# A later gate group's last plain unit becomes a seventh Strassen unit, and the turned results get their low parts from ScalarE and adding transfers

## The chip, the cores and the metric

The kernel runs on one core of one Trainium2 chip. The metric is the time of the program on the device, in microseconds (us), as the median of several runs. The profile is one further execution, recorded by the hardware profiler. The engines are called by the profile's names: PE (TensorE: matmuls; PEld is its weight load), DVE (VectorE), ACT (ScalarE), POOL (GpSimd, here mostly a place from which transfers are issued) and SP (SyncE, which issues the loads).

## The reference, cut to what matters

One layer of a decoder trunk: 256 tokens, width 2048, all numbers float32. The change touches only the feed-forward part, of width `D_FF` = 5632:

```
f = rmsnorm(h, ffn_norm[i])
h = h + (jax.nn.silu(f @ w_gate[i]) * (f @ w_up[i])) @ w_down[i]
```

Ahead of it stand an input projection, two kinds of attention and an output projection; behind it a gated embedding (`w_ple_gate`, `w_ple_proj`) and a last norm.

## The kernel before, in words

**Products in three matmuls.** Each factor is split into a high part (the number rounded to the fp32r type) and a low part (what the rounding left). A product is three matmuls: high by high, low by high, high by low (`three`, L385). The low part of a weight block is read by the third alone. The high part of a weight block is cast by ScalarE (L337), the low part is made by VectorE as raw minus high (L348).

**Groups and units.** The feed-forward part goes through six chunks of 1024 columns of `w_gate` and `w_up`. For each chunk there is a gate group (`g0` to `g4`), an up group (`u0` to `u4`) and, one chunk later, two groups of `w_down` (`d1` to `d4`, each for half of the output columns, which I write d20 and d21 for chunk 2). The sixth chunk is narrower and does gate and up in one group, `gu5`. The order is g0, u0, g1, d10, u1, d11, g2, d20, u2, d21, g3 and so on to d41, gu5, and then the last two groups of `w_down`. A group is a list of units, each of 256 rows of the weight (a *pair* of 128-row tiles), 1024 columns wide.

**Plain and Strassen units.** A plain unit is 2 row tiles x 2 column chunks x 2 token tiles x 3 = 24 matmuls of 128x512. A unit marked `S` in `mixed` (L1080) does the same in seven block products instead of eight (Strassen's scheme in Winograd's form): 7 x 3 = 21 matmuls, in four *turns* of 6, 3, 6 and 6 (`seven`, L442). It needs the four blocks of the weight and four sums of them: VectorE makes the sums in place (L347, L350, L351) and low parts of seven blocks instead of four. The blocks are named "11 22", "21", "t1 t3" and "t4 t2": two, one, two and two blocks of 512 columns, one name for each turn. Within turn 0 they are used by products m1 and m3, in turn 1 by m2, in turn 2 by m7 and m5, in turn 3 by m6 and m4. Three of the seven (m2, m3, m4) add straight to the result banks (0,0), (1,0) and (0,1), where the plain units' products lie too, as they do in the fourth, (1,1); m1, m5, m6 and m7 have a bank each, and VectorE puts them together in the tile `U` after the last Strassen unit (L465 to L469).

**Order before.** `mixed` lists the units: `6 S0 S1 S2 S3 S4 S5 7` for g1 to g4 and gu5, `S0 S1 S2 S3 S4 S5 S6 7` for u1 to u4. The four result banks are copied to the tile `stage` by ScalarE after the last plain unit (`gate_add`, L1012), and an adding transfer from POOL adds `U` to them (L1018).

**The ring.** Casted blocks live in 20 places of 512 columns (12 in `ring`, 4 in `more`, 4 in `most`), filled in turn; `plan` (L232) gives each block its place and notes which turn last reads it. A block must not straddle places 12 or 16. The main loop (L1382 to L1425) issues the casts of later units before each turn's matmuls, as far ahead as the loads, three units at most, and the ring allow: a block whose place is read by turn n is issued at turn n + 1 at the earliest. `high_parts` issues ScalarE's casts, then `step` runs one piece of each waiting task, then `split` issues the rest. Each engine carries its instructions out in the order in which they are issued.

**The middle of the first plain unit.** The chunk's result (gate times up, in `stage`) has to be turned before `w_down` can use it. This is done in the first plain unit of the next gate group: half of the unit's matmuls, then 16 transposes on PE into the four spare banks (`ff_transpose`, L1041), then the other half. Before, each bank was cast by ScalarE (L106) and its low part taken by VectorE (L107), and the four banks were then free for m1, m7, m5, m6 of the first Strassen unit. Blocks that could have been issued ahead of this (`late`) were issued behind it.

Of the kernel before, what the change touches and what calls it, by code (L numbers as in the profile page):

```python
# [13 lines left out]
ALU = mybir.AluOpType  # L14
# [21 lines left out]
def kernel(ctx, tc, x, w_in, w_ukv, w_o, w_gate, w_up, w_down, w_ple_gate, w_ple_proj,  # L36
# [137 lines left out]
    def group(name, srcs, ks, chunks, lhs, evac, pool=None, singles=0, per=2, sums=None, sevens=(), adding=(),  # L174
              order=None, swap=False, bank0=0, deep=False, into=None, early=(), keep=False):

        pairs = [ks[i:i + 1] for i in range(singles)] + [ks[i:i + per] for i in range(singles, len(ks), per)]
        st = {"banks": None, "begun": set()}
        for i, pr in enumerate(pairs):
            u = Unit()  # L180
            u.name, u.srcs, u.ks, u.chunks, u.lhs, u.st = name, srcs, pr, chunks, lhs, st
            u.first, u.last, u.evac, u.pool = i == 0, i == len(pairs) - 1, evac, pool
            u.order = order or [(c, t) for c in range(len(chunks)) for t in range(NT)]
            u.idx, u.store, u.again, u.into = i, None, None, into
            u.strassen, u.sevens_first, u.sevens_end = i in sevens, i in sevens[:1], i in sevens[-1:]
            u.mixed, u.sums, u.swap, u.bank0, u.deep, u.adding = len(sevens) > 0, sums, swap, bank0, deep, i in adding
            u.early, u.keep = i in early, keep
            units.append(u)

    raw = {}  # L190
# [213 lines left out]
    def product(u, kks, between=()):  # L404

        end = u.last and kks[-1] == len(u.ks) - 1
        take_banks(u)
        parts = u.parts if not u.again else units[u.again].parts
        for c, t in u.order:
            if c == "keys":  # L410
                b = u.st["banks"][c, t]
                for kk in kks:
                    for i in range(2):
                        w = [x[:, (2 * t + i) * 128:(2 * t + i + 1) * 128] for x in parts[kk]]
                        three(b[:, i * SEQ:(i + 1) * SEQ], w, *(x[:, u.ks[kk], :] for x in S["ckvT"]),
                              begins(u, (c, t)), end and kk == kks[-1] and i == 1)
                if end:
                    u.evac(c, t, 0, 512, b)
                continue
            c0, c1 = u.chunks[c]  # L420
            b = u.st["banks"][c, t][:, 0:c1 - c0]
            for kk in kks:
                h, l = parts[kk]
                three(b, u.lhs(u.ks[kk], t), h[:, c0:c1], l[:, c0:c1], begins(u, (c, t)), end and kk == kks[-1])
            if end:
                if u.mixed and u.into is None and not isinstance(u.evac, partial):
                    us = S["U"][:, t, c0:c1]
                    nc.vector.tensor_tensor(us, us, b, op=ALU.add)
                    u.evac(c, t, c0, c1, us)
                else:  # L430
                    u.evac(c, t, c0, c1, b)
                if between and (c, t) == u.order[0]:
                    split(between.pop(0))
        if end and u.mixed and not u.keep:
            B["acc"], B["rot"], B["next"] = u.st["free"], [u.st["banks"][ct] for ct in u.order], 0
        elif end and u.swap:
            swap_banks()
# [4 lines left out]
    def seven(u, turn):  # L442
        st = u.st
        if turn == 0 and u.sevens_first:
            take_banks(u)
            n = B["next"] % 4
            st["free"] = B["rot"][n:] + B["rot"][:n]
            B["rot"], B["next"] = [st["banks"][1, 1]] if u.first else [], 0
            st.update(zip(("m1", "m7", "m5", "m6"), st["free"]))
        h, l = u.turns[turn][0].h, u.turns[turn][0].l  # L450
        k = u.ks[0]
        a11, a12, a22 = u.lhs(k, 0), u.lhs(k + 1, 0), u.lhs(k + 1, 1)
        s1, s2, s3, s4 = (u.sums(k, j) for j in range(4))
        todo = (((0, "m1", a11), (1, "m3", s4)), ((0, "m2", a12),), ((1, "m7", s3), (0, "m5", s1)),
                ((1, "m6", s2), (0, "m4", a22)))[turn]
        alone = {"m2": (0, 0), "m3": (1, 0), "m4": (0, 1)}
        for q, m, xs in todo:
            b = st["banks"][alone[m]] if m in alone else st[m]
            three(b, xs, h[:, 512 * q:512 * q + 512], l[:, 512 * q:512 * q + 512], begins(u, alone.get(m, m)),
                  u.sevens_end and m not in alone)  # L460
        if turn == 3 and u.sevens_end:
            U = S["U"] = big.tile([128, NT, 1024], F32, name="U", tag="vb")
            c1, c2 = U[:, :, 0:512], U[:, :, 512:1024]
            tt = nc.vector.tensor_tensor
            nc.scalar.copy(c1[:, 0], st["m1"])  # L465
            tt(c2[:, 0], c1[:, 0], st["m6"], op=ALU.add)
            tt(c1[:, 1], c2[:, 0], st["m7"], op=ALU.add)
            tt(c2[:, 0], c2[:, 0], st["m5"], op=ALU.add)
            tt(c2[:, 1], c1[:, 1], st["m5"], op=ALU.add)  # L469
            B["rot"], B["next"] = st["free"], 0  # L470
            if u.into is not None:
                def join(hs=S["h"][:, :, u.into:u.into + 1024]):
                    tt(hs, hs, U, op=ALU.add)
                    yield 1
                add(join())
# [536 lines left out]
    def gate_add(ci, c, t, c0, c1, b):  # L1012

        if "ff" not in S:
            S["ff"] = stage_tile(1024)
        nc.scalar.copy(S["ff"][:, t, c0:c1], b)
        if (c, t) == (1, 1):
            nc.gpsimd.dma_start(S["ff"], S["U"], accum_op=ALU.add)  # L1018

            def silu():  # L1020
                for i in range(NT):
                    nc.scalar.activation(S["ff"][:, i], S["ff"][:, i], AF.Silu, scale=S["rf"][:, i:i + 1])
                yield 1
            add(silu(), 4)

    def up_evac(ci, n, nb):
        left = {"n": nb}
# [13 lines left out]
    def ff_transpose(ci, n, st):  # L1041
        if ci == 5:
            ft = big.tile([128, 2, 6, SEQ], F32R, name="ffT", tag="att")
            tl = ffT[ci] = [ft[:, 0], ft[:, 1]]
        else:
            tl = ffT[ci] = parts_tile("ffT", "f0")
        lows = []
        for k in range(0, n // 128, 2):
            b = obank()
            for i in range(2):  # L1050
                for t in range(NT):
                    nc.tensor.transpose(b[:, (2 * i + t) * 128:(2 * i + t + 1) * 128],  # L1052
                                        st[:, t, (k + i) * 128:(k + i + 1) * 128], ident)
            h, l, f = tl[0][:, k:k + 2, :], tl[1][:, k:k + 2, :], b.rearrange("q (a s) -> q a s", a=2)
            if ci or k < 4:
                split_psum(h, l, f)
            else:
                kept = st[:, :, k * 128:(k + 2) * 128]
                nc.scalar.copy(kept, f)
                lows.append((l, kept, h))  # L1060
                nc.scalar.copy(h, kept)
            if k % 4 == 2:
                yield 1

        def low_parts():
            for l, kept, h in lows:
                nc.vector.tensor_tensor(l, kept, h.bitcast(F32), op=ALU.subtract)
            yield 1
        if lows:
            add(low_parts(), 11, True)  # L1070

    def ff_l(k, t):
        ci, kk = divmod(k, 8)
# [5 lines left out]

    def mixed(name, order=((0, 0), (1, 0), (0, 1), (1, 1))):  # L1080

        pairs = {'g0': '0 1 2 3 4 5 6 7', 'u0': '6 S0 S1 S2 S3 S4 7 5', 'g1': '6 S0 S1 S2 S3 S4 S5 7'}.get(
            name, '6 S0 S1 S2 S3 S4 S5 7' if name[0] == 'g' else 'S0 S1 S2 S3 S4 S5 S6 7').split()
        n = [int(x.strip("S+")) for x in pairs]
        sevens = tuple(i for i, x in enumerate(pairs) if x[0] == "S")
        return dict(ks=[2 * x + i for x in n for i in range(2)], chunks=C2, lhs=a_l, sums=a_sums, sevens=sevens,
# [262 lines left out]
    for i, u in enumerate(units):  # L1349
# [32 lines left out]
        for n in range(max(1, len(u.turns))):  # L1382
# [7 lines left out]
                todo.append(jobs[nxt])  # L1390
                nxt += 1
            weave = u.name in WOVEN and u.last
            if "mid" in S and not u.strassen and u.mixed or u.sevens_end and u.name != "u0" and n == 3 or weave:
                late = [jb for jb in todo if jb.turn > j]
                todo = [jb for jb in todo if jb.turn <= j]
            if i >= 5:
                high_parts(todo + late if weave or "mid" in S and units[i + 1].early else todo)
            if i == 2:
                product(u, [0])
            if n % 2 == 0:  # L1400
# [13 lines left out]
            else:  # L1414
                product(u, [kk for jb in u.turns[n] for kk in jb.kks] if u.turns else range(len(u.ks)), late if weave else ())
            if "mid" in S and not u.strassen and u.mixed:
                while units[i + 1].early and late and late[0].unit == i + 1:
                    split(late.pop(0))
                for _ in S.pop("mid"):
                    pass  # L1420
# [35 lines left out]
```

## Time and profile before

| | |
|---|---|
| runs, median | 1177.69 us (3 runs, 1177.53 to 1178.32) |
| profiled execution | 1178.31 us |
| its span, first to last instruction | 1176.5 us |
| granted TensorE clock | 0.998 |
| PE busy | 1165.2 us |
| DVE busy | 975.5 us |
| ACT busy | 717.7 us |

The span is the time between the first and the last instruction of the profiled execution, whose own time on the device is 1.8 us more. Busy shares are means over the whole span; the part that the change touches, from g1 to the end of gu5, lies between 456 and 1012 us of it. A line of a timeline gives the start, the duration, the engine, the line of the kernel, the operation, its output and inputs with their shapes, the number of such instructions in a row, and in square brackets how long the engine was idle before and what ended the idle time.

### The profile page before, as it was taken

To read this page: it belongs to the slowest core of one execution; us is meant where nothing else is said; L and a number is where in the kernel's file an instruction comes from. 1 tells how busy PE (TensorE), PEld (TensorE's weight loads), DVE (VectorE), ACT (ScalarE), POOL (GpSimd) and SP (SyncE) were. 2 spreads that over 40 slices of the span, in tenths; PEclk is the share of its full clock that TensorE was granted. 3 is DMA by queue.
4 is the path that set the end of the run, shared out by engine and by line. 5 is a ranking of instruction groups with operands and counts; after the bars stand their busy time and mean duration, and the time that the engine had idled before them with its cause. 6 is when DMAs were issued, how large, how long until landed. Compare 5 with 4: busy or idle time off the path is not lost.

```text
span 1176.5 us, 14646 instructions
## 1 busy us (share of the span) xinstructions
PE 1165.2 (99%) x5468; PEld 975.9 (83%) x5468; DVE 975.5 (83%) x1168; ACT 717.7 (61%) x917; POOL 50.8 (4%) x74
## 2 busy tenths in 40 slices
PE   9999999999999999999999999999999999999996
PEld 6888888899888888888888888888888888888886
DVE  6866756776557679999999899989998999898984
ACT  6745746456456766667566665668475756465563
POOL 5000000000000000000000000000000000000000
PEclk9999999999999999999999999999999999999999
DMA  9896787755684777686968697778868795836441
GB/s 327 296 343 201 291 298 257 268 186 204 220 331 130 273 260 284 241 278 211 352 180 278 174 352 217 228 232 331 230 219 260 264 285 192 340 141 218 166 156 72
DMA packets 85881, 287.81 MB, mean 245 GB/s; under 512 B 5681, under 2 KB 7985, under 8 KB 81201
## 3 DMA queue, kind: packets, MB, share of 16 engines
q1 hardware_dynamic: 76208, 238.66, 56.3%
q0 software_dynamic: 9024, 47.19, 14.5%
q10 hardware_dynamic: 576, 1.02, 0.3%
q8 instruction: 43, 0.70, 0.2%
q14 instruction: 30, 0.24, 0.1%
HBM read 252.24 MB, written 26.21 MB: 237 GB/s over the span
## 4 chain that ended last, share of the span: by engine, by line
PE 98%; DMA 1%; DVE 0%; ACT 0%; DVEq 0%; issue 0%
PE bank L390 31%; PE bank L388 31%; PE bank L389 31%; PE bank L591 1%; DMA raw<-in_w_in 1%; PE bank L1052 1%; PE bank L123 1%; PE bank L620 1%; PE bank L614 0%; PE bank L594 0%; PE bank L726 0%; PE bank L621 0%; PE bank L751 0%; ACT ringh L337 0%; DVE h L1268 0%; ACT stage L1216 0%
## 5 line engine op out<-in xcount | busy, mean ns | idle before, releaser
L337 ACT CAST ringh<-raw 128x1024 fp32r<-128x1024 f32 (+4 forms) x320 | 374.4, 1208 | 263.5 <-DVE raw L347 94.4
L348 DVE TENSOR_TENSOR ringl<-raw,ringh 128x1024 fp32r<-128x1024 f32 (+4 forms) x320 | 446.2, 1418 | 79.3 <-ACT ringh L337 77.3
L388 PE MATMUL bank<-ringh,aT 128*128 128x512 f32 (+3 forms) x688 | 264.4, 384 | 0.3
L390 PE MATMUL bank<-ringl,aT 128*128 128x512 f32 (+3 forms) x688 | 261.1, 380 | 0.1
L389 PE MATMUL bank<-ringh,aT 128*128 128x512 f32 (+3 forms) x688 | 260.4, 378 | 0.0
L390 PEld LDWEIGHTS bank<-ringl,aT 128*128 128x128 f32 x688 | 129.2, 188 | 25.0 <-DVE ringl L348 1.8
L388 PEld LDWEIGHTS bank<-ringh,aT 128*128 128x128 f32 x688 | 129.3, 188 | 23.8 <-ACT ringh L337 1.5
L389 PEld LDWEIGHTS bank<-ringh,aT 128*128 128x128 f32 x688 | 129.4, 188 | 22.8 <-DVE aT L658 0.3
L337 ACT CAST moreh<-raw 128x1024 fp32r<-128x1024 f32 (+2 forms) x74 | 83.7, 1166 | 19.5 <-DVE raw L347 9.2
L348 DVE TENSOR_TENSOR morel<-raw,moreh 128x1024 fp32r<-128x1024 f32 (+2 forms) x70 | 90.2, 1311 | 3.6 <-ACT moreh L337 3.1
L388 PE MATMUL bank<-ringh,ffTh 128*128 128x512 f32 x204 | 79.5, 390 | 0.0
L390 PE MATMUL bank<-ringl,ffTh 128*128 128x512 f32 x204 | 79.4, 389 | 0.0
L389 PE MATMUL bank<-ringh,ffTl 128*128 128x512 f32 x204 | 79.4, 389 | 0.0
L337 ACT CAST most<-raw 128x1024 fp32r<-128x1024 f32 (+2 forms) x58 | 57.0, 1007 | 34.3 <-DVE raw L347 16.7
L347 DVE TENSOR_TENSOR raw<-raw 128x1024 f32<-128x1024 f32 x54 | 66.2, 1225 | 1.8
L348 DVE TENSOR_TENSOR most<-raw,most 128x1024 fp32r<-128x1024 f32 (+2 forms) x58 | 66.7, 1163 | 0.2
L390 PEld LDWEIGHTS bank<-ringl,ffTh 128*128 128x128 f32 x204 | 38.3, 188 | 8.0
L388 PEld LDWEIGHTS bank<-ringh,ffTh 128*128 128x128 f32 x204 | 38.3, 188 | 7.9
L389 PEld LDWEIGHTS bank<-ringh,ffTl 128*128 128x128 f32 x204 | 38.3, 188 | 7.9
L351 DVE TENSOR_TENSOR raw<-raw 128x512 f32<-128x512 f32 x54 | 37.4, 692 | 1.9
L350 DVE TENSOR_TENSOR raw<-raw 128x512 f32<-128x512 f32 x54 | 37.0, 684 | 0.0
L388 PE MATMUL bank<-most,aT 128*128 128x512 f32 x88 | 34.6, 394 | 0.0
(373 smaller groups left out, 2009.2 us busy)
## 6 DMA issues: line engine op xcount, KB each, us to landing
raw<-in_w_down SPq DMA_DIRECT2D x44, 1024.0 KB, 6.8
raw<-in_w_gate SPq DMA_DIRECT2D x37, 1024.0 KB, 7.7
raw<-in_w_up SPq DMA_DIRECT2D x30, 1024.0 KB, 8.0
raw<-in_w_in SPq DMA_DIRECT2D x40, 512.0 KB, 5.2
raw<-in_w_o SPq DMA_DIRECT2D x16, 1024.0 KB, 6.1
raw<-in_w_ple_gate SPq DMA_DIRECT2D x16, 1024.0 KB, 5.1
wsums<-in_w_up POOLq DMA_DIRECT2D x10, 1024.0 KB, 7.6
wsumsu<-wsums POOLq DMA_DIRECT2D x10, 1024.0 KB, 4.7
```

Source lines behind the costliest of these rows:

```text
L123: nc.tensor.transpose(b[:, (2 * i + t) * 128:(2 * i + t + 1) * 128], part[:, t, i * 128:(i + 1) * 128], ident)
L337: nc.scalar.copy(h[:, :, c0:c1], r[:, :, c0:c1])
L347: tt(f[:, 0:2], f[:, 1:2].to_broadcast([128, 2, 512]), f[:, 0:4:3], op=ALU.subtract)
L348: tt(l[:, :, c0:c1], r[:, :, c0:c1], h[:, :, c0:c1].bitcast(F32), op=ALU.subtract)
L350: tt(f[:, 3], f[:, 3], f[:, 0], op=ALU.subtract)
L351: tt(f[:, 2], f[:, 2], f[:, 3], op=ALU.subtract)
L388: nc.tensor.matmul(b, xh, h, start=start, stop=False)
L389: nc.tensor.matmul(b, xl, h, start=False, stop=False)
L390: nc.tensor.matmul(b, xh, l, start=False, stop=stop)
L591: nc.tensor.matmul(s[:, c0:c0 + nk], qT[:, q * 128:(q + 1) * 128], kT[:, 0:nk], start=True, stop=qpe is None)
L620: nc.tensor.matmul(o[:, 0:256], v(0), pT[:, 0:256], start=True, stop=False)
L1052: nc.tensor.transpose(b[:, (2 * i + t) * 128:(2 * i + t + 1) * 128], st[:, t, (k + i) * 128:(k + i + 1) * 128], ident)
```

## The change

In g2, g3 and g4 the list becomes `7 S0 S1 S2 S3 S4 S5 S6`: the plain unit comes first and there are seven Strassen units. g1 and gu5 keep their lists. As no plain unit follows the last Strassen unit, that unit ends the group: ScalarE copies m1's bank to `U` and the result banks (1,1) and (1,0) to `stage` after its turn 0, bank (0,0) after turn 1, bank (0,1) after turn 3, and the adding transfer follows VectorE's sums (`gate_sum`). The blocks of the next units that fall to turn 3 are then issued ahead of those sums and no longer behind them. The next group takes the four result banks in the order in which they were copied.

For the turned results of chunks 1 to 4, ScalarE copies each bank back to `stage` as it is, and VectorE has nothing to do there. Later (`by_transfer`, first piece two calls of `step` after the transposes, one piece a call) ScalarE makes the high parts in two copies of 1024 columns, then writes minus the value to the low tile in two pieces of 1024 columns, and a transfer from POOL adds the value itself to each. In the first unit of g2, g3, g4 and gu5 the blocks in `late` are now issued ahead of the transposes.

```diff
@@ mixed
-        pairs = {..., 'g1': '6 S0 S1 S2 S3 S4 S5 7'}.get(
-            name, '6 S0 S1 S2 S3 S4 S5 7' if name[0] == 'g' else 'S0 S1 S2 S3 S4 S5 S6 7').split()
+        pairs = {..., 'g1': '6 S0 S1 S2 S3 S4 S5 7', 'gu5': '6 S0 S1 S2 S3 S4 S5 7'}.get(
+            name, '7 S0 S1 S2 S3 S4 S5 S6' if name[0] == 'g' else 'S0 S1 S2 S3 S4 S5 S6 7').split()
@@ seven
             three(b, xs, h[:, 512 * q:512 * q + 512], l[:, 512 * q:512 * q + 512], begins(u, alone.get(m, m)),
-                  u.sevens_end and m not in alone)
+                  u.sevens_end and (u.last or m not in alone))
+        if u.sevens_end and turn == (0 if u.last else 3):
+            S["U"] = big.tile([128, NT, 1024], F32, name="U", tag="vb")
+            nc.scalar.copy(S["U"][:, 0, 0:512], st["m1"])
+        for c, t in (((1, 1), (1, 0)), ((0, 0),), (), ((0, 1),))[turn] if u.last else ():
+            u.evac(c, t, *u.chunks[c], st["banks"][c, t])
         if turn == 3 and u.sevens_end:
...
             B["rot"], B["next"] = st["free"], 0
+            if u.last:
+                gate_sum()
+                B["acc"] = [st["banks"][ct] for ct in ((1, 1), (1, 0), (0, 0), (0, 1))]
@@ ff_transpose
-            if ci or k < 4:
+            if ci in (1, 2, 3, 4):
+                nc.scalar.copy(st[:, :, k * 128:(k + 2) * 128], f)
+            elif ci or k < 4:
                 split_psum(h, l, f)
...
+        def by_transfer():
+            v = st.rearrange("q a (m s) -> q m a s", s=SEQ)
+            h, l = (x.rearrange("q (m a) s -> q m a s", a=2) for x in tl)
+            for a in range(2):
+                nc.scalar.copy(h[:, :, a], v[:, :, a])
+                yield 1
+            for a in range(2):
+                nc.scalar.mul(l[:, :, a], v[:, :, a], -1.0)
+                nc.gpsimd.dma_start(l[:, :, a], v[:, :, a], accum_op=ALU.add)
+                yield 1
         if lows:
             add(low_parts(), 11, True)
+        elif ci < 5:
+            add(by_transfer(), 2)
@@ main loop
-            if "mid" in S and not u.strassen and u.mixed or u.sevens_end and u.name != "u0" and n == 3 or weave:
+            if "mid" in S and not u.strassen and u.mixed or u.sevens_end and u.name != "u0" and n == 3 and not u.last or weave:
                 late = [jb for jb in todo if jb.turn > j]
                 todo = [jb for jb in todo if jb.turn <= j]
             if i >= 5:
-                high_parts(todo + late if weave or "mid" in S and units[i + 1].early else todo)
+                high_parts(todo + late if weave or "mid" in S and (units[i + 1].early or u.name != "g1") else todo)
...
             if "mid" in S and not u.strassen and u.mixed:
-                while units[i + 1].early and late and late[0].unit == i + 1:
+                while late and (u.name != "g1" or units[i + 1].early and late[0].unit == i + 1):
                     split(late.pop(0))
                 for _ in S.pop("mid"):
                     pass
```

More of the change, by code (lines that the diff above doesn't have):

```diff
@@ L187, in group @@
             u.early, u.keep = i in early, keep
+            u.ends = i not in sevens and all(x in sevens for x in range(i + 1, len(pairs)))
             units.append(u)
@@ L423, in product @@
                 h, l = parts[kk]
-                three(b, u.lhs(u.ks[kk], t), h[:, c0:c1], l[:, c0:c1], begins(u, (c, t)), end and kk == kks[-1])
+                done = end or u.ends and (c, t) == (1, 1) and kks[-1] == len(u.ks) - 1
+                three(b, u.lhs(u.ks[kk], t), h[:, c0:c1], l[:, c0:c1], begins(u, (c, t)), done and kk == kks[-1])
             if end:
@@ L433, in product @@
                     split(between.pop(0))
+        if end and u.mixed and isinstance(u.evac, partial):
+            gate_sum()
         if end and u.mixed and not u.keep:
@@ L459, in seven @@
             three(b, xs, h[:, 512 * q:512 * q + 512], l[:, 512 * q:512 * q + 512], begins(u, alone.get(m, m)),
-                  u.sevens_end and m not in alone)
+                  u.sevens_end and (u.last or m not in alone))
[4 more added lines that the diff above has]
+            u.evac(c, t, *u.chunks[c], st["banks"][c, t])
         if turn == 3 and u.sevens_end:
-            U = S["U"] = big.tile([128, NT, 1024], F32, name="U", tag="vb")
+            U = S["U"]
             c1, c2 = U[:, :, 0:512], U[:, :, 512:1024]
             tt = nc.vector.tensor_tensor
-            nc.scalar.copy(c1[:, 0], st["m1"])
             tt(c2[:, 0], c1[:, 0], st["m6"], op=ALU.add)
@@ L470, in seven @@
             B["rot"], B["next"] = st["free"], 0
+            if u.last:
+                gate_sum()
+                B["acc"] = [st["banks"][ct] for ct in ((1, 1), (1, 0), (0, 0), (0, 1))]
             if u.into is not None:
@@ L1016, in gate_add, with gate_sum, silu @@
         nc.scalar.copy(S["ff"][:, t, c0:c1], b)
[L1017 to L1024, printed above, removed]
+    def gate_sum():
+        nc.gpsimd.dma_start(S["ff"], S["U"], accum_op=ALU.add)
+        def silu():
+            for i in range(NT):
+                nc.scalar.activation(S["ff"][:, i], S["ff"][:, i], AF.Silu, scale=S["rf"][:, i:i + 1])
+            yield 1
+        add(silu(), 4)
     def up_evac(ci, n, nb):
@@ L1068, in low_parts @@
             yield 1
+        def by_transfer():
[7 more added lines that the diff above has]
+                nc.gpsimd.dma_start(l[:, :, a], v[:, :, a], accum_op=ALU.add)
+                yield 1
         if lows:
             add(low_parts(), 11, True)
+        elif ci < 5:
+            add(by_transfer(), 2)
     def ff_l(k, t):
@@ L1080, in mixed @@
     def mixed(name, order=((0, 0), (1, 0), (0, 1), (1, 1))):
-        pairs = {'g0': '0 1 2 3 4 5 6 7', 'u0': '6 S0 S1 S2 S3 S4 7 5', 'g1': '6 S0 S1 S2 S3 S4 S5 7'}.get(
-            name, '6 S0 S1 S2 S3 S4 S5 7' if name[0] == 'g' else 'S0 S1 S2 S3 S4 S5 S6 7').split()
+        pairs = {'g0': '0 1 2 3 4 5 6 7', 'u0': '6 S0 S1 S2 S3 S4 7 5', 'g1': '6 S0 S1 S2 S3 S4 S5 7', 'gu5': '6 S0 S1 S2 S3 S4 S5 7'}.get(
+            name, '7 S0 S1 S2 S3 S4 S5 S6' if name[0] == 'g' else 'S0 S1 S2 S3 S4 S5 S6 7').split()
         n = [int(x.strip("S+")) for x in pairs]
```

## The prediction

> **What bounds the kernel now.** First the page's head and the weight loader's waits: is anything but PE's own work on the path?
>
> ```profile
> span 1176.5 us, 14646 instructions
> ...
> PE 1165.2 (99%) x5468; PEld 975.9 (83%) x5468; DVE 975.5 (83%) x1168; ACT 717.7 (61%) x917; POOL 50.8 (4%) x74
> ```
> ```profile
> PEld bank L390 <- DVE ringl L348: 1.8, 6, 0.4
> ```
>
> PE is busy throughout; its waits for low parts come to 1.8 us. So a matmul taken away is time won, unless a new wait eats it. The chain of waits gives the groups' rhythm by their transposes:
>
> ```profile
> 592.14 1.75 PE bank L1052 x16
> 715.79 1.75 PE bank L1052 x16
> 839.45 1.75 PE bank L1052 x16
> 963.14 1.75 PE bank L1052 x16
> ```
>
> g2, g3, g4 and gu5 begin 123.65 us apart, so I work on g2's clock for all. Next the windows: 592 to 632 is g2 from the transposes on.
>
> ```profile
> 592.00:632.00 40.00, 40.00 (x186) 33.18 (x185) 37.97 (x41) 26.68 (x31) 0.63 (x1) 1.00 0.62 193
> ```
>
> The columns after the length are PE, PEld, DVE and ACT: VectorE 37.97 of 40 us busy, ScalarE 26.68, DMA share 0.62. Then VectorE's and ScalarE's timelines:
>
> ```profile
> 589.85 1.22 DVE L348 TENSOR_TENSOR ringl<-raw,ringh 128x1024 fp32r<-128x1024 f32 x1
> 593.24 2.48 DVE L107 TENSOR_TENSOR ffTl<-bank,ffTh 128x512 fp32r<-128x512 f32 x4 [2.16 <-ACT ffTh L106]
> 595.64 2.36 DVE L348 TENSOR_TENSOR morel<-raw,moreh 128x1024 fp32r<-128x1024 f32 x2
> 598.04 1.23 DVE L347 TENSOR_TENSOR raw<-raw 128x1024 f32<-128x1024 f32 x1
> ...
> 604.79 1.22 DVE L347 TENSOR_TENSOR raw<-raw 128x1024 f32<-128x1024 f32 x1
> 605.93 0.68 DVE L348 TENSOR_TENSOR ringl<-raw,ringh 128x512 fp32r<-128x512 f32 x1
> 606.53 0.68 DVE L350 TENSOR_TENSOR raw<-raw 128x512 f32<-128x512 f32 x1
> 607.25 0.69 DVE L351 TENSOR_TENSOR raw<-raw 128x512 f32<-128x512 f32 x1
> 607.86 3.64 DVE L348 TENSOR_TENSOR ringl<-raw,ringh 128x1024 fp32r<-128x1024 f32 x3
> 611.54 1.23 DVE L347 TENSOR_TENSOR raw<-raw 128x1024 f32<-128x1024 f32 x1
> ...
> 621.36 4.78 DVE L348 TENSOR_TENSOR ringl<-raw,ringh 128x1024 fp32r<-128x1024 f32 x4
> 626.35 2.29 DVE L348 TENSOR_TENSOR ringl<-raw,ringh 128x2048 fp32r<-128x2048 f32 x1 [0.21 <-ACT ringh L337]
> 628.56 0.68 DVE L466 TENSOR_TENSOR U<-U,bank 128x512 f32<-128x512 f32 x1
> ```
> ```profile
> 589.05 2.04 ACT L934 COPY copied<-bank 128x512 f32<-128x512 f32 x4
> 592.62 2.06 ACT L106 CAST ffTh<-bank 128x512 fp32r<-128x512 f32 x4 [1.53 <-PE bank L1052]
> 594.53 2.03 ACT L337 CAST moreh<-raw 128x1024 fp32r<-128x1024 f32 x2
> ...
> 606.12 1.05 ACT L337 CAST ringh<-raw 128x1024 fp32r<-128x1024 f32 x1 [2.29 <-DVE raw L347]
> 608.05 2.53 ACT L337 CAST ringh<-raw 128x1024 fp32r<-128x1024 f32 x3 [0.88 <-DVE raw L351]
> ```
>
> From L347 at 604.79 (S3's) to the next unit's at 611.54, VectorE spends 6.75 us on a Strassen unit. PE's timeline shows what PE takes:
>
> ```profile
> 601.25 0.39 PE L388 MATMUL bank<-ringh,aT 128*128 128x512 f32 x1
> ...
> 606.01 0.39 PE L388 MATMUL bank<-moreh,aT 128*128 128x512 f32 x1
> ...
> 630.62 0.39 PE L388 MATMUL bank<-ringh,ffTh 128*128 128x512 f32 x1
> ```
> ```profile
> 626.19 0.19 PEld L390 LDWEIGHTS bank<-ringl,aT 128*128 128x128 f32 x1 [0.24 <-DVE ringl L348]
> ```
>
> S1 begins at 601.25 and S2 at 606.01: 21 matmuls in 4.76 us, 0.2267 us each. VectorE loses 2.0 us per Strassen unit, living off its head start. At 626.19, in the closing plain unit, the loader waits for the low part that ends at 626.14 (621.36 + 4.78): the head start is exactly used up. Work of VectorE, not matmuls, is scarce at just this place.
>
> **The change part by part.**
>
> *Matmuls.* 3 in each of 3 groups: 9 x 0.2267 = 2.04 us less. The old wait at 626.19 goes too; the unit took 5.53 us (625.09 to 630.62) for 24 x 0.2267 = 5.44, so that is 0.09 a group. The most that can be won is 2.4 us (9 matmuls, four such waits).
>
> *VectorE's bill.* The closing unit costs 6.75 instead of about 2.4 us (two blocks of 1.2, in the row at 621.36): 4.35 more. The four L107 (2.48 us) go, and the 2.16 us idle before them may. If all of that were usable, the head start would last: 4.64 against 4.35, and 0.7 us because PE comes sooner.
>
> *How much of the 4.64 us is usable, in g2.* Order on ScalarE: bank copies to 591.09, the casts of the two late blocks (S1's "t4 t2", S2's "11 22") to 593.05, then the four copies of turned banks (0.51 each) to 595.1, then S2's "21". VectorE makes the late blocks at 592.2 instead of 595.64. Then the ring stops it: S2's "t1 t3" takes places that the plain unit's second half reads until 596.6, S3's "11 22" places that S0's turn 2 reads until 600.0; its cast ends at 601.2. VectorE reaches L347 of S3 at 602.5 instead of 604.79: 2.25 us won, not 4.64.
>
> *In g3, g4 and gu5 the ring has moved.* g2 now takes 53 places instead of 50. Counting on by the planner's rule, the last unit of d21 sits in places 0 to 3, and S1's "t1 t3" falls to 0 and 1 (before: 10 and 11, cast ahead of the bank copies). So it cannot be cast before PE leaves d21, and the row at 589.85, which is that block, moves behind the copies. The late blocks become S1's last two (VectorE 592.2 to 594.6); S2's "11 22" is issued behind the turned banks' copies and its cast ends at 596.2. VectorE idles 1.65 us, starts S2's L347 at 597.5 instead of 598.04 and S3's, after two small waits, at 604.4: 0.4 us won instead of 2.25. g4 and gu5 come out alike (S1's "t1 t3" behind d31's and d41's last unit).
>
> *ScalarE's pieces of by_transfer.* Four instructions of 128x1024, 1.05 us (row at 606.12), issued at turns 0 and 2 of S1 and of S2. In turn 0 they fall into ScalarE's 2.29 us idle before "t1 t3" (cover gone: up to 1 us each). In turn 2 they stand between the cast of "t4 t2" and that of the next "11 22". The row at 608.05 shows these casts back to back, 0.97 apart. From L351's end at t = 0.7 (counted from its start): cast at 0.80, piece at 1.77, next cast 2.74 to 3.79; VectorE wants that block at 3.06 and gets it at 3.87: 0.8 us. Queued behind the piece are all later casts, and behind those VectorE. Twice in g2, g3 and gu5; in g4 once, since there S5's "11 22" is issued ahead of the piece. The bounds of this price: 0, if ScalarE has caught up by then, and 1.05. I take 0.8, as the rows give it.
>
> *Where it ends.* Unhindered, S5 starts at 601.25 + 4 x 4.76 = 620.29, S6 at 625.05, d's first unit (d.a) at 629.81. "t1 t3" is first needed 11 matmuls into a unit; by the row at 626.19 a low part must be ready 0.16 before its matmul. That is 622.6 for S5, 627.4 for S6, 630.1 for d.a. VectorE ends "t1 t3" 4.29 us after the unit's L347 (604.79 to 607.86, and 1.22), d.a's low part 3.45 us later (1.2 and 2.25).
> - g2: S5's L347 at 602.5 + 13.5 + 1.6 (waits; 0.2 for one more small one) = 617.8; S6's "t1 t3" ready at 628.85, 1.45 late; d.a at 632.3 against 630.1 + 1.45, 0.75 late. d.a comes at 629.81 + 2.2, against 630.62: +1.4 us.
> - g3: L347 at 604.4 + 13.5 + 1.6 = 619.5; S5 late by 1.2, S6 by 2.0, d.a by 0.75: 3.95 late, +3.15.
> - g4: one piece less: 618.7; 0.4, 1.95 and 0.75 late: +2.3.
> - gu5, which keeps its closing plain unit: S5 late by 1.2, the plain unit by 0.25, less the old 0.09: +1.35.
>
> Sum +8.2 us, the matmuls already counted in it: 1178.3 + 8.2 = 1186.5 for the profiled execution, which lay 0.6 above the median; so **1185.9**.
>
> *The rest, at nothing.* d's other units come with slack: VectorE idles in the next row for 2.80 us at d20's end, which takes up most of its lateness (PE is late by as much), so that u starts with the head start it had.
>
> ```profile
> 654.14 1.23 DVE L348 TENSOR_TENSOR ringl<-raw,ringh 128x1024 fp32r<-128x1024 f32 x1 [2.80 <-ACT ringh L337]
> ```
> ```profile
> stage<-U POOLq DMA_DIRECT2D x4, 1024.0 KB, 8.9
> morel<-raw POOLq DMA_DIRECT2D x4, 1024.0 KB, 11.5
> ```
>
> Without that slack u would inherit up to 2.4 us a group. by_transfer's transfers (512 KB each) are issued by POOL at about 613 and 617, in front of nothing until `gate_sum`; d.a needs them at 630. Even at 11.5 us, the time of twice the data, they land by 629. `gate_sum` goes out some 8 to 10 us later than before, behind three splits and U's sums, and lands about 2 us ahead of the copies at d20's end, which write the same memory; a cost of 0 to 2 us a group that I take as 0. The bank copies during S6 keep ScalarE from nothing urgent: d.a and d.b are cast ahead of them. Their banks come free before d uses them.
>
> **The rivals.**
> - *Only the ring costs* (ScalarE's pieces hidden): g2 -0.25, g3 and g4 +1.5 each, gu5 -0.1: +2.65, 1180.3. For it: ScalarE's 26.68 us of 40; against: the row at 608.05, where it runs without a gap.
> - *VectorE keeps its head start* (the other side): if the low part of S6's "t1 t3" is ready by 627.4 in all three groups, which needs the idle 1.65 us and the pieces' 0.8 us filled, PE never waits: -2.4 us, 1175.3. For it: 4.64 us freed against 4.35 + 0.7; against: the order of the casts, which lets none of it be saved up.
> - *Gains and waits cancel*, between these two: about 1177.7.
> - *A wait slows PE's clock.* The window row grants 1.00, with waits under 0.4 us; no row shows what 2 us would do. If the waits worked out above (2.2, 3.95, 3.1 and 1.45 us) cost as much again, 10.7 us more: 1196.6. [...]
> - *by_transfer lands late* for d.a (two transfers of 11.5 us behind one another): up to 5 us in each of three groups, from the point at which the second takes over 13 us; some 1190 with half of that.
>
> **How the numbers follow.** Forecast 0.45, ring alone 0.2, head start kept 0.17, cancelling 0.13, the last two 0.05 together. What can be told from no change is 0.2%, 2.36 us: 1175.3 to 1180.05. The head start's case lies on that edge, so it goes in halves and a little: faster 0.12; same 0.22 (the rest of it, cancelling, a little of the ring's case); slower 0.66. The likeliest case alone, by its bounds (pieces at 0.5 to 1.05), spans 1182 to 1189. The range goes down to the head start's case: 1175.2 to 1189.
>
> **What would show it.** Right: the loader's waits for L348 in S5, S6 and d.a grow from 0.2 to 2 to 4 us a group, in g3 more than in g2; VectorE idle before S2's first block in g3, not g2; VectorE waiting for ScalarE's cast right behind by_transfer's pieces in S1 and S2. Wrong: PE without waits from 592 to 1012 and groups 0.7 us closer together; or transfers, not low parts, as what ends PE's waits.

## The result and the profile after

The kernel after takes 1192.52 us (median of 4 runs, 1191.26 to 1192.84) against 1177.61 for the kernel before beside it: ratio 1.0123, 95% interval 1.0106 to 1.0141. It is 14.9 us slower, where 8.2 were predicted, and 3.5 us above the upper end of the predicted range (1175.2 to 1189). In what follows line numbers are those of the kernel after, which are a few higher from L337 on (the cast L337 is now L338, the low part L348 now L349, the sums L347, L350 and L351 now L348, L351 and L352; gate_sum's copies of the result banks to `stage` are L1027, the transposes L1065, by_transfer's pieces L1089 and L1092).

The head of the page of the kernel after:

```profile
span 1190.3 us, 14715 instructions
...
PE 1169.5 (98%) x5459; PEld 975.9 (82%) x5459; DVE 980.4 (82%) x1167; ACT 737.9 (62%) x939; POOL 61.0 (5%) x82
```

The nine matmuls are gone (5459 for 5468). PE's busy time rises all the same, by 4.3 us; where that comes from is told below. The chain of waits has the transposes at which g2, g3, g4 and gu5 begin:

```profile
591.87 1.75 PE bank L1065 x16
719.56 1.75 PE bank L1065 x16
848.91 1.75 PE bank L1065 x16
976.54 1.75 PE bank L1065 x16
```

They were 123.65 us apart and are now 127.69, 129.35 and 127.63 apart: +4.0, +5.7 and +4.0. From gu5 to the end it is 0.4 us more, up to g2 0.3 less. These make up the span's 13.8 us. So the loss lies in the three groups that got the seventh unit. What the weight loader waited for, summed over the span (total, times, longest; 0.9 us of the second row lies ahead of g1):

```profile
PEld bank L389 <- ACT stage L1027: 7.3, 3, 2.4
PEld bank L391 <- DVE ringl L349: 4.5, 6, 1.6
PEld bank L391 <- DVE most L349: 2.2, 3, 1.6
PEld bank L389 <- ACT copied L945: 1.3, 2, 1.0
```

And where the large ones are, in the loader's timeline (`sums6h` is a factor of S6, `ffTh` one of the first unit of d, which the prediction calls d.a):

```profile
628.05 0.19 PEld L391 LDWEIGHTS bank<-ringl,sums6h 128*128 128x128 f32 x1 [1.04 <-DVE ringl L349]
632.64 0.19 PEld L389 LDWEIGHTS bank<-moreh,ffTh 128*128 128x128 f32 x1 [2.44 <-ACT stage L1027]
...
757.16 0.19 PEld L391 LDWEIGHTS bank<-most,sums6h 128*128 128x128 f32 x1 [1.61 <-DVE most L349]
761.76 0.19 PEld L389 LDWEIGHTS bank<-ringh,ffTh 128*128 128x128 f32 x1 [2.45 <-ACT stage L1027]
...
885.75 0.19 PEld L391 LDWEIGHTS bank<-ringl,sums6h 128*128 128x128 f32 x1 [1.61 <-DVE ringl L349]
890.34 0.19 PEld L389 LDWEIGHTS bank<-moreh,ffTh 128*128 128x128 f32 x1 [2.44 <-ACT stage L1027]
```

Each group has a wait for a low part in S6, as forecast, and 4.6 us later a longer one at d.a's first matmul, for ScalarE: not for a cast, but for a copy that frees a result bank. ScalarE's timeline in g2 shows why that copy is late:

```profile
626.97 1.05 ACT L338 CAST ringh<-raw 128x1024 fp32r<-128x1024 f32 x1 [0.88 <-DVE raw L352]
627.92 1.90 ACT L338 CAST moreh<-raw 128x2048 fp32r<-128x2048 f32 x1
629.73 1.90 ACT L338 CAST most<-raw 128x2048 fp32r<-128x2048 f32 x1
631.52 0.58 ACT L467 COPY U<-bank 128x512 f32<-128x512 f32 x1
632.00 1.56 ACT L1027 COPY stage<-bank 128x512 f32<-128x512 f32 x3
```

S6's "t4 t2" can't be cast before VectorE has made its sum (L352); the casts of d.a and of the unit behind it (d.b) stand behind that, and the bank copies behind all three. They begin at 631.52, and d.a's first matmul starts at 632.64, just behind the first of the three `stage` copies, which ends at 632.6. VectorE's lateness thus reaches PE a second time, by way of ScalarE's queue and the banks.

The last part is the clock. Windows of 2 us behind these waits (length; busy PE, PEld, DVE, ACT and POOL; granted clock; DMA share; GB/s):

```profile
634.00:636.00 2.00, 2.00 (x6) 1.61 (x5) 0.95 (x2) 2.00 (x3) 0.00 (x0) 0.50 0.96 385
764.00:766.00 2.00, 2.00 (x7) 1.54 (x6) 1.48 (x1) 2.00 (x3) 0.00 (x0) 0.50 1.01 403
892.00:894.00 2.00, 2.00 (x10) 1.63 (x10) 0.95 (x2) 2.00 (x3) 0.00 (x0) 1.00 1.01 408
```

After the waits in g2 and g3 PE ran at half clock, matmuls 0.43 us apart; after the one in g4 it did not. PE's timeline gives the price:

```profile
632.64 0.50 PE L389 MATMUL bank<-moreh,ffTh 128*128 128x512 f32 x1 [2.00 <-ACT stage L1027]
...
636.86 0.39 PE L391 MATMUL bank<-morel,ffTh 128*128 128x512 f32 x1
...
890.34 0.50 PE L389 MATMUL bank<-moreh,ffTh 128*128 128x512 f32 x1 [2.02 <-ACT stage L1027]
...
892.99 0.39 PE L391 MATMUL bank<-morel,ffTh 128*128 128x512 f32 x1
```

From d.a's first matmul to the eleventh behind it are 4.22 us in g2 and 2.65 in g4: 1.6 us for each halving, 3.2 for two. PE itself idled 2.00 and 2.02 us where the loader's row says 2.44: in g2 the loader ends at 630.20 and the matmul ahead of the wait at 630.64. So the first part of each wait, 0.44 us in g2, counts as busy time of PE. Together with the 3.2 us this is why PE's busy time rose.

The sum: matmuls -2.0, the old waits -0.3, bank waits 7.3, low parts 5.8 and late casts of ScalarE 0.6 (6.4 together), copies at u's start 1.3, clock 3.2, together 15.9. The loader's lists run some 0.15 us a wait above what PE loses: at d.a in g2 the second matmul starts 2.28 us later than it would without the wait, where the loader's row says 2.44. For the 14 waits over 0.2 us that is 2.1, which leaves the 13.8 measured.

### The profile page after: what moved, and what is told of

The parts are those of the page before. It is cut to its first block, busy times and chain, and to the rows that moved or that the text cites. A ratio compares the mean times of both kernels' runs of the same rounds, so it can differ in the third digit from the quotient of the medians.

```text
span 1190.3 us, 14715 instructions
## 1 busy us (share of the span) xinstructions
PE 1169.5 (98%) x5459; PEld 975.9 (82%) x5459; DVE 980.4 (82%) x1167; ACT 737.9 (62%) x939; POOL 61.0 (5%) x82
## 4 chain that ended last, share of the span: by engine, by line
PE 92%; DVE 3%; ACT 2%; issue 2%; DMA 0%; ACTq 0%; DVEq 0%; SPq 0%
PE bank L391 29%; PE bank L389 29%; PE bank L390 29%; DVE ringl L349 1%; PE bank L602 1%; PE bank L1065 1%; ACT ringh L338 1%; PE bank L123 1%; ACT moreh L338 1%; PE bank L631 1%; PE bank L625 0%; PE bank L737 0%; PE bank L605 0%; DVE raw L348 0%; DVE raw L352 0%
## 5 line engine op out<-in xcount | busy, mean ns | idle before, releaser
L338 ACT CAST ringh<-raw 128x1024 fp32r<-128x1024 f32 (+4 forms) x322 | 377.1, 1205 | 237.1 <-PE bank L390 82.5
L349 DVE TENSOR_TENSOR ringl<-raw,ringh 128x1024 fp32r<-128x1024 f32 (+5 forms) x319 | 442.5, 1407 | 87.1 <-ACT ringh L338 85.4
L338 ACT CAST moreh<-raw 128x1024 fp32r<-128x1024 f32 (+2 forms) x78 | 85.4, 1127 | 46.0 <-DVE raw L348 29.8
L349 DVE TENSOR_TENSOR morel<-raw,moreh 128x1024 fp32r<-128x1024 f32 (+2 forms) x77 | 98.9, 1304 | 10.8 <-ACT moreh L338 10.2
L338 ACT CAST most<-raw 128x1024 fp32r<-128x1024 f32 (+2 forms) x58 | 58.8, 1036 | 28.7 <-DVE raw L348 15.6
L389 PE MATMUL bank<-ringh,ffTh 128*128 128x512 f32 x180 | 71.0, 394 | 2.0 <-ACT stage L1027 2.0
L348 DVE TENSOR_TENSOR raw<-raw 128x1024 f32<-128x1024 f32 x57 | 69.8, 1225 | 2.0
L349 DVE TENSOR_TENSOR most<-raw,most 128x1024 fp32r<-128x1024 f32 (+2 forms) x58 | 69.1, 1202 | 2.2 <-ACT most L338 1.9
L391 PE MATMUL bank<-ringl,ffTh 128*128 128x512 f32 x180 | 70.8, 393 | 0.0
L390 PE MATMUL bank<-ringh,ffTl 128*128 128x512 f32 x180 | 70.6, 392 | 0.0
L389 PEld LDWEIGHTS bank<-ringh,ffTh 128*128 128x128 f32 x180 | 34.2, 190 | 9.5 <-ACT stage L1027 2.4
L389 PE MATMUL bank<-moreh,aT 128*128 128x512 f32 x105 | 41.3, 393 | 0.0
L352 DVE TENSOR_TENSOR raw<-raw 128x512 f32<-128x512 f32 x57 | 39.4, 692 | 2.0
L391 PE MATMUL bank<-morel,aT 128*128 128x512 f32 x105 | 40.9, 390 | 0.0
L390 PE MATMUL bank<-moreh,aT 128*128 128x512 f32 x105 | 40.9, 389 | 0.0
L390 PEld LDWEIGHTS bank<-ringh,ffTl 128*128 128x128 f32 x180 | 34.2, 190 | 7.1
```

The costliest lines, as they stand in the source:

```text
L338: nc.scalar.copy(h[:, :, c0:c1], r[:, :, c0:c1])
L348: tt(f[:, 0:2], f[:, 1:2].to_broadcast([128, 2, 512]), f[:, 0:4:3], op=ALU.subtract)
L349: tt(l[:, :, c0:c1], r[:, :, c0:c1], h[:, :, c0:c1].bitcast(F32), op=ALU.subtract)
L352: tt(f[:, 2], f[:, 2], f[:, 3], op=ALU.subtract)
L389: nc.tensor.matmul(b, xh, h, start=start, stop=False)
L390: nc.tensor.matmul(b, xl, h, start=False, stop=False)
```

## The experiments

Theory A: the seventh Strassen unit makes VectorE late, and this lateness is the root of all the waits, the bank copies' too. The rivals (B) put the loss on something else that the change brought: ScalarE's pieces and the transfers, the casts' new order, the place of the bank copies. The diffs are against the kernel after.

**The old lists, with all else of the change.**

```diff
-            name, '7 S0 S1 S2 S3 S4 S5 S6' if name[0] == 'g' else ...
+            name, '6 S0 S1 S2 S3 S4 S5 7' if name[0] == 'g' else ...
```

> One part alone: the unit lists of g2, g3 and g4 as before (plain unit 6 first, plain unit 7 last), everything else of the change kept: by_transfer, the late blocks ahead of the transposes. Theory A (the seventh Strassen unit at the end of the group makes nearly all of the loss, because VectorE comes late and ScalarE's bank copies stand behind its casts): within 0.3% of the kernel before, 1176 to 1181 us, no wait of PE for the copies to stage, and groups 123 to 124.5 us apart as gu5's 0.4 us of loss in the changed kernel suggests. Theory C (by_transfer's pieces and its small transfers make most of it): 1184 us or more.

Measured: 1177.3 us, ratio 0.9995 (0.9985 to 1.0004). The loader has no wait over 0.3 us from g1 to the end of gu5, and the three groups between these rows of the chain take 123.49 us each:

```profile
591.86 1.75 PE bank L1065 x16
...
962.34 1.75 PE bank L1065 x16
```

So by_transfer and the order of the late blocks cost nothing by themselves. All 14.9 us come with the seventh unit.

**Seven units, but low parts of the turned results by VectorE as before.**

```diff
@@ ff_transpose
-            if ci in (1, 2, 3, 4):
+            if False:
                 nc.scalar.copy(st[:, :, k * 128:(k + 2) * 128], f)
...
-        elif ci < 5:
-            add(by_transfer(), 2)
```

> The other part alone: seven units in g2, g3, g4, but the turned results cast and split by ScalarE and VectorE straight from the banks as before. Theory A: VectorE pays 2.48 us a group at the transposes and gets back the two waits of 0.67 us behind by_transfer's pieces, so it comes some 1.1 us later to the last unit than in the changed kernel: 1194 to 1198 us. Theory C: clearly faster than the changed kernel, under 1187 us.

Measured: 1189.54 us, ratio 1.0099 (1.0083 to 1.0114). This lies between the two ranges and is a miss: 3 us *faster* than the kernel after, where A expected it slower. Its waits:

```profile
PEld bank L389 <- ACT stage L1027: 7.3, 3, 2.5
PEld bank L391 <- DVE ringl L349: 3.0, 4, 1.2
PEld bank L389 <- ACT copied L945: 2.0, 1, 2.0
```

The bank wait is the same, but S6 waits 1.20, 1.01 and 1.00 us, alike in all three groups, and g3's S5 and gu5 no longer wait. Handing back to VectorE the four low parts (2.48 us a group) makes it hardly later: S6's first sum in g2 starts at 624.04 instead of 623.70, and g2 itself 0.18 later. In the kernel after, VectorE idles soon behind the transposes for ScalarE's casts (0.56 and 0.82 us in g2) and twice more behind by_transfer's pieces (0.67 each); here these four waits are gone. So the time that the change frees for VectorE is lost again before the group's end. The two halves of the change do not pay for each other.

**ScalarE's pieces at turn 0 of S0 to S3**, where its queue has room, no more at turns 0 and 2 of S1 and S2.

```diff
@@ by_transfer (both places)
-                yield 1
+                yield 2
...
-            add(by_transfer(), 2)
+            add(by_transfer(), 0)
```

> The changed kernel, with by_transfer's four pieces at turn 0 of S0, S1, S2 and S3 instead of at turns 0 and 2 of S1 and S2. If the two waits of VectorE of 0.67 us a group come from the pieces at turn 2, they go, VectorE and with it ScalarE's last casts come 1.3 us earlier, in gu5 too: PE's waits for low parts and for the copies shrink by about that in each of g2, g3, g4: 1187.5 to 1189.5 us. If the pieces' place is of no matter: 1191 to 1193 us.

Measured: 1187.9 us, ratio 1.0084 (1.0069 to 1.0099), as expected. In g2 the wait in S6 is gone and the one for the banks is shorter:

```profile
630.69 0.19 PEld L389 LDWEIGHTS bank<-moreh,ffTh 128*128 128x128 f32 x1 [1.81 <-ACT stage L1027]
```

In g3 and g4 S6 waits 0.92 and 0.91 and the banks 2.45 and 2.44; the clock halves once, in g3. The pieces' place is worth 4.6 us; two thirds of the loss stay.

**Bank copies ahead of d.b's cast**, by holding that cast back until S6's last turn.

```diff
@@ main loop, the condition on which blocks are issued
+                    not (i + 1 < len(units) and units[i + 1].sevens_end and units[i + 1].last and jobs[nxt].unit > i + 2) and \
```

> The changed kernel, with the cast of the second unit of w_down held back until the last turn of the closing Strassen unit, so that it no longer stands ahead of the bank copies on ScalarE (1.81 us earlier copies). Theory A: the wait of 2.44 us for the copies shrinks, but the first w_down unit's own low part, ready at about 1.5 us after PE wants it, takes its place: 0.9 us a group won, 1189 to 1190.5 us. Theory B (the copies alone are the wait): about 1.8 us a group, 1185.5 to 1187.5 us.

Measured: 1194.28 us, ratio 1.0138 (1.0121 to 1.0155): a miss. It is 1.8 us above the kernel after, where both theories expected less.

```profile
PEld bank L389 <- ACT copied L945: 7.6, 3, 3.2
...
PEld bank L389 <- ACT stage L1027: 2.6, 6, 0.7
```

The bank wait falls from 2.44 to 0.63 to 0.67 at d.a. In its place d.a's own low part is 1.06 late in each group (the forecast had 0.75), and at the end of d20, d30 and d40 the same thing happens again with d's banks: 2.21, 3.17 and 2.18 us for `copied`. At d20's end these copies follow a cast that waited for VectorE's sum (L352). So the copies' place at d.a is not the root: when they are moved there, the lateness comes out at the next place, 24 us on.

**S6 without its three sums**, so 2.6 us a group less for VectorE; queues and order are unchanged. These units compute with the unsummed blocks. The second of the two kernels has the pieces spread as above too.

```diff
@@ split_lo
-        f = quarters(jb) if jb.kind == "21" and not units[jb.unit].early else None
+        f = quarters(jb) if jb.kind == "21" and not units[jb.unit].early and \
+            not (units[jb.unit].sevens_end and units[jb.unit].last) else None
```

> The kernel after, but the three sums of the weight blocks that VectorE makes for the last unit of g2, g3 and g4 (L348, L351, L352: 1.23 + 0.69 + 0.69 = 2.6 us a group) are left out, so these three units use the unsummed blocks. Everything else, the order of casts and bank copies included, is as in the kernel after. Theory A (VectorE's lateness is the root of all three kinds of wait): the loader's waits at S6 (1.04, 1.61, 1.61) and at d.a for the bank copies (2.44 in each group) fall under 0.5, those at g3's S5 (0.48, 0.28) stay since they come before; g2 and g4 last about 122.9 us, g3 about 123.7; 1176 to 1179, no halved clock. Theory B (the bank copies' place in ScalarE's queue or the banks' order costs by itself): the waits at d.a stay over 1.5 us in each group; 1184 to 1188.

> The same three sums left out, and by_transfer's pieces at turn 0 of S0 to S3 as in the run with spread pieces (1187.9). Theory A: no wait over 0.5 us from 456 to 1012 but a copied one at u's start of up to 1 us; groups 122.9 apart; 1175 to 1177.5, which is the rival of the kept head start (1175.3) and all that seven units can win. Theory B: the waits at d.a (1.81, 2.45, 2.44 there) stay over 1.5; 1182 to 1186.

Measured: 1181.22 us, ratio 1.0026 (1.0017 to 1.0036), and with spread pieces 1177.51, ratio 0.9999 (0.9989 to 1.0008). The first, with its waits:

```profile
PEld bank L389 <- ACT copied L945: 3.8, 3, 2.0
PEld bank L389 <- ACT stage L1027: 1.7, 2, 1.0
```

No order was touched, and yet the bank wait goes from 2.44 in each group to 0, 1.03 and 0.65, S6 waits no more, and the clock is 1.00 throughout the feed-forward part: 7.8 us of VectorE's work less, 11.3 us of time less. That decides for A and against B, which kept over 1.5 us in each group. But leaving the sums out does two things: it takes work from VectorE, and it frees ScalarE's casts of S6 from waiting for VectorE. How much each of them is worth was not separated. Two of the bank waits stay above the 0.5 us that A expected, and the time is 2 us above its range, mostly since ScalarE's copies at u's start were late (0.88, 1.97 and 0.97). With spread pieces only these are left (1.73 and 0.76, where up to 1 was expected), the time is at the upper edge of its range, and g2 has no wait, as the chain shows:

```profile
591.43 1.75 PE bank L1065 x16
714.24 1.75 PE bank L1065 x16
838.66 1.75 PE bank L1065 x16
```

g2 lasts 122.81 us, 0.68 less than the 123.49 of the old lists, which is three matmuls (3 x 0.2267). g3 lasts 124.42, and the two timelines at its u's start show the same coupling a third time:

```profile
772.58 1.99 ACT L338 CAST moreh<-raw 128x1024 fp32r<-128x1024 f32 x2 [0.95 <-DVE raw L352]
774.48 2.04 ACT L945 COPY copied<-bank 128x512 f32<-128x512 f32 x4
```
```profile
775.11 0.19 PEld L389 LDWEIGHTS bank<-ringh,aT 128*128 128x128 f32 x1 [1.73 <-ACT copied L945]
```

**S6's sums made early instead of left out.** The kernel makes some weight sums in its first part and keeps them in memory; here S6 of g2, g3 and g4 are added to these, with the early sums started at smaller distances so that they fit; pieces spread.

```diff
-    EARLY = dict(..., u1=(5, 6), u2=(5, 6), u3=(5, 6), u4=(5, 6))
+    EARLY = dict(..., u1=(5, 6), g2=(6,), u2=(5, 6), g3=(6,), u3=(5, 6), g4=(6,), u4=(5, 6))
...
-            add(early_sums("f0l", 2, lambda: 53248, raw[i + 3][:, 0, 0:1]))
+            add(early_sums("f0l", 2, lambda: 40960, raw[i + 3][:, 0, 0:1]))
...
-            add(early_sums("more_sums", 99, lambda: 57344 if S["long"] else 34816))
+            add(early_sums("more_sums", 99, lambda: 40960 if S["long"] else 24576))
```

> by_transfer's pieces spread as in the run before, and VectorE relieved at just the closing unit: its block sums of g2's, g3's and g4's S6 are made in the first half of the kernel, as those of 13 other units are (the sums there stand closer together for it), and come in by a load. VectorE spends 4.2 us instead of 6.75 on S6, and ScalarE's casts of S6 no longer wait for VectorE. Theory A (VectorE's lateness at S6 is the root, of the low parts and, over ScalarE's queue, of the bank copies): no wait over 0.5 us at S6 or at the first unit of w_down, no halved clock, and the nine matmuls show: 1174.5 to 1177 us, if the first half takes the sums for nothing. Theory B (the copies stand behind the casts of w_down's first two units whatever VectorE does): waits of 1.5 to 2.4 us stay at the first unit of w_down: 1181 to 1185 us.

Measured: 1203.4 us, ratio 1.0207 (1.0193 to 1.0221), a miss in the total. The chain and one row of the loader's timeline:

```profile
494.89 1.75 PE bank L1065 x16
618.44 1.75 PE bank L1065 x16
741.27 1.75 PE bank L1065 x16
```
```profile
281.21 0.29 PEld L391 LDWEIGHTS bank<-ringl,aT 128*128 128x128 f32 x1 [7.90 <-DVE ringl L349]
```

The first transposes come at 494.89 instead of 468.29: the whole loss is made in the first part, where the denser early sums hold up the weights' low parts. Ahead of the row shown, VectorE idles 8.91 us for the load of an early sum's weights, and the low part stands behind that sum. From g2 on no group waits in S6 or at d.a, and g2 lasts 122.83 us; behind d30 and d40 `copied` is late by 1.74 and 1.13. So the same holds with a right result: give VectorE room, and the seventh unit saves its three matmuls.

**Fewer of them: seven units in g3 and g4, or in g4 alone**, each with S6's sums made early, pieces spread; for g4 alone the early sums keep their old distances.

```diff
-            name, '7 S0 S1 S2 S3 S4 S5 S6' if name[0] == 'g' else ...
+            name, '7 S0 S1 S2 S3 S4 S5 S6' if name in ('g3', 'g4') else '6 S0 S1 S2 S3 S4 S5 7' if name[0] == 'g' else ...
...
-    EARLY = dict(...)
+    EARLY = dict(..., g3=(6,), g4=(6,))
...
-            add(early_sums("more_sums", 99, lambda: 57344 if S["long"] else 34816))
+            add(early_sums("more_sums", 99, lambda: 57344 if S["long"] else 30720))
```

> The relief of the last run where it may be had more cheaply: seven Strassen units in g3 and g4 alone, the block sums of these two closing units made in the first half (15 such units instead of 16, at nearly the old pace), the pieces of by_transfer spread. If VectorE's lateness is the root and the first half takes two more units for nothing: 6 matmuls, 1.4 us, less a wait of up to 1.7 us at the start of u4, as the last run had in its g3 and g4: 1176 to 1178 us. If the first half still pays: over 1180 us.

> The same with g4 alone (14 such units at the old pace): 3 matmuls, 0.7 us, no wait at the closing unit or behind it, and a first half as in the kernel before: 1176 to 1177.5 us, the same as the kernel before or just below it. If a closing Strassen unit makes PE wait whatever VectorE does: g4 and d40 take over 2 us more, 1179 us or more.

Measured: 1184.83 us, ratio 1.0062 (1.0048 to 1.0076), and 1183.3, ratio 1.0047 (1.0034 to 1.0059). Both came out dear. For the first that is the branch in which the first part still pays; behind it g3 lasts 122.84 us, and g4, with the expected wait at u4 (1.72), 124.47. For g4 alone the time falls into the range of the dear branch, but not for its reason, a wait in g4 or d40: there is none, and the miss is the first part, which was expected to cost nothing. The chain:

```profile
474.25 1.75 PE bank L1065 x16
...
844.87 1.75 PE bank L1065 x16
967.71 1.75 PE bank L1065 x16
```

g4 lasts 122.84 us and the others 123.52 to 123.58. But the first transposes are 6.0 us later than in the kernel after (468.29), for a single early sum, and ScalarE's and PE's timelines name the place:

```profile
379.71 0.62 ACT L106 CAST sumsmore_sums<-stage 128x512 fp32r<-128x512 f32 x1 [8.09 <-DMA wsumsu<-wsums]
```
```profile
383.31 0.50 PE L391 MATMUL bank<-morel,aT 128*128 128x512 f32 x1 [2.88 <-DVE morel L349]
```

A cast of ScalarE waits, after 8.09 us of idleness, for the transfer that carries the last early sum away. VectorE stands behind that cast, PE waits 2.88 us for it, and the clock is at 0.50 for the 3.4 us that follow. No kernel here is faster than the one before by more than the noise.

**A dose of lateness by itself**: the old lists, and 8, 13 and 19 idle additions on VectorE ahead of the first low part of d20, d30 and d40.

```diff
@@ main loop
+                for _ in range(DOSE.get(units[jb.unit].name, 0) if units[jb.unit].idx == 0 else 0):
+                    jk = work.tile([128, 512], BF, name="junk", tag="junk")
+                    nc.vector.memset(jk, 0.0) if _ == 0 else nc.vector.tensor_tensor(jk, pj, pj, op=ALU.add)
+                    pj = jk
```

> What one wait costs by itself: the unit lists as before (no wait of PE there), by_transfer kept, and ahead of the low part of the first w_down unit of chunk 2, 3 and 4 VectorE does 8, 13 and 19 idle additions of 512 numbers (they change no result). They delay that low part, and PE waits once, for some 2, 4 and 7 us if an addition takes 0.5 us. If the halved clock follows from the length of a wait alone, it comes after the waits over some 2 to 2.5 us, for about 3.4 us. If it needs two waits close together, it does not come after the first of the three.

Measured: 1189.12 us, one run. PE's waits in d20 stay near 0.5 us; in d30 and d40 they are

```profile
757.06 0.19 PEld L391 LDWEIGHTS bank<-ringl,ffTh 128*128 128x128 f32 x1 [2.44 <-DVE ringl L349]
887.65 0.19 PEld L391 LDWEIGHTS bank<-ringl,ffTh 128*128 128x128 f32 x1 [5.20 <-DVE ringl L349]
```

and the granted clock behind both is 0.50 for 3.4 us (windows of 2 us that the stretch fills in part show 0.62 and 0.53, and 0.55 and 0.60). So the halved clock came here without the seventh unit, without bank copies and without a second long wait close by; behind the wait in d30, for a low part, PE had idled 2.02 us.

## Why the prediction was right in direction and too small

- *PE bounds the kernel and a matmul taken away is 0.2267 us won*: right. Where the seventh unit brought no new wait (g2 with spread pieces and S6's sums left out or made early, g4 alone) the group lasts 0.7 us less than with the old lists.
- *VectorE's head start is used up at the group's end, and the seventh unit asks 4.35 us more*: right, and the root of the loss (S6 without its sums: -11.3 us).
- *Only 2.25 of the 4.64 us freed can be used in g2*: about right. VectorE's timeline of the kernel after has S3's sum at 601.98 for 602.5 forecast, of which 0.27 is g2's earlier start. It shows the pieces' price too, 0.67 us twice for the 0.8 taken; S5's sum came at 616.95 for 617.8.

```profile
601.98 1.22 DVE L348 TENSOR_TENSOR raw<-raw 128x1024 f32<-128x1024 f32 x1
...
608.21 1.23 DVE L349 TENSOR_TENSOR ringl<-raw,ringh 128x1024 fp32r<-128x1024 f32 x1 [0.67 <-ACT ringh L338]
...
615.69 1.23 DVE L349 TENSOR_TENSOR most<-raw,most 128x1024 fp32r<-128x1024 f32 x1 [0.67 <-ACT most L338]
...
723.06 1.23 DVE L349 TENSOR_TENSOR ringl<-raw,ringh 128x1024 fp32r<-128x1024 f32 x1 [2.27 <-ACT ringh L338]
```

- *The ring moves in g3, so VectorE idles 1.65 us*: seen, 2.27 us in the last row. But as a term of its own it was too large: without the pieces g3 and g4 wait no more in S6 than g2. Low parts and late casts came to 1.04, 2.75 and 1.85 us in g2, g3 and g4 for 1.45, 3.2 and 2.35 forecast, and gu5 waits 0.74 for 1.45: 6.4 for 8.45.
- *"The bank copies during S6 keep ScalarE from nothing urgent: d.a and d.b are cast ahead of them. Their banks come free before d uses them."* **This is the step that failed.** It looked at what the copies hold up and took it that they themselves are not held up. The casts ahead of them wait for VectorE's sum, whose delay the forecast had worked out, and take 1.05 and twice 1.90 us; so d.a waits 2.44 us for its bank in place of 0.75 for its low part: 7.3 for 2.25 us. The same step fails again at the ends of d30 and d40: there `copied` stands in the same queue behind casts, and PE waits 0.35 and 0.97 us for it, for which the sum had no term. (The 0 taken of 0 to 2 us there was for something else, the landing of `gate_sum`, and it held: the copies follow the casts ahead of them without a pause for it.)
- *The clock*, held to 1.00 with a chance of 0.05 shared with another rival: it halved in two groups of three, 3.2 us, less than a third of the rival's 10.7, because only waits at d.a did it, and not all of these. Ahead of these two halvings PE had idled 2.00 and 2.02 us, and 2.02 in the group without one. That waits of such a length leave the clock at 1.00 was the author's estimate; the kernel before has no such wait from 20 to 1020 us.
- *by_transfer's transfers land in time*: right, 5.4 to 11.0 us from issue to landing, and PE waits for none of them.

In sum: low parts -2.1 against the forecast, banks +5.1, copies at u's start +1.3, clock +3.2, and -2.1 for the loader's surplus on 14 waits: 5.4 of the 5.6 us by which the profiled span missed the 8.2.

The rivals of no change and of a gain needed VectorE's time at the transposes to be usable at the group's end; the run without transfers shows that giving it back changes little there (S6's first sum in g2 0.34 us later). What remains open is why, in the kernel after and in the run with spread pieces and no sums, d20's end has no wait while d30's and d40's have one; the ring's places differ, but no run varied these alone.

## What to carry to other kernels

Trading matmuls for another engine's work pays only if that engine has time free in just that stretch; ask where the time freed lies, not how much it is. When a copy that frees a bank, or anything else that PE needs, is put behind other work in an engine's queue, price it by what stands ahead of it there and by what these instructions wait for (here 4.55 us of ScalarE's casts, from 626.97 to the copy at 631.52, and VectorE's sum ahead of them). And a wait of PE like those of 2.00 to 2.04 us here should be counted with the chance of a halved clock behind it: six of these nine had one.

## What the runs showed of the hardware

What the granted clock did behind PE's waits is told by the runs' timelines of PE, from 20 to 1020 us. Of 9 stretches in which PE idled between 1.30 and 1.79 us, none was followed by a halved clock; of 9 between 2.00 and 2.04, six were (two of three in the kernel after, two of three in the run without transfers, one of two with spread pieces, and the dose in d30); of 7 from 2.75 to 7.64, all were. Its length is told by the windows of 2 us: what they lack of 1.00, taken as time at 0.50, comes to 3.4 us in ten of the 13 cases (in the kernel after 0.83, 0.50 and 0.82 from 632 on: 0.68 + 2.0 + 0.72) and to 6.8, twice that, in the other three, all behind long waits of the first part (5.76 and 7.64 us in the run with S6's sums made early, 2.84 in the one with seven units in g3 and g4). Nine waits of 2.00 to 2.04 us with unequal outcomes mean that in these runs the wait's length alone did not decide.

The same windows tell when the clock fell. In the kernel after it fell at 633.32 (634 less the 0.68) and, by the 0.76 granted from 762 to 764, at 763.04: 0.68 and 1.28 us after PE's waits in g2 and g3 had ended. What decides between waits of equal length was not shown: no run here moved a wait and left all else as it was.
